# A new order for the 52 tiles of the first input projection

## The chip, the cores and the metric

The kernel runs on one core of a Trainium2 chip. The metric is the device time of one execution in microseconds (us). The engines are named as in the profile: PE is the matrix engine (PEld its weight loads), DVE, ACT and POOL are the vector, scalar and general engines, SP issues the DMAs.

## What is computed

One inference step of a decoder trunk of two layers, for 512 prompt tokens and 8 x 4 sample tokens (544 columns in all), model width 2048. The first layer, in which the change lies:

```
h = x @ w_in
h_sh, gate_a, q_b, k_b, v_b, gate_b, q_m, gate_m = _split(
    h, (A_SHIFT_W, A_WIDTH, B_WIDTH, B_WIDTH, B_WIDTH, B_OUT, M_WIDTH, M_WIDTH))
y_a, s_new = rwkv7_mix(h_sh + (prev - h_sh) * mu, s0, ...)
y_b = combine_by_denominator(outs, lses)      # dilated window attention, 3 groups x 4 heads
y_m = memory_attention(q_m, mkv)              # 4 heads, 256 memory tokens
u = concat([y_a * silu(gate_a), y_b * silu(gate_b), y_m * silu(gate_m)])
x = layer_norm(ALPHA * x + u @ w_out, ln_g, ln_b)
```

The recurrence of rwkv7_mix (12 heads x 64) runs in pairs of heads, so there are six pairs. The second layer (retention and the same memory attention) has a projection, heads and an output projection of its own.

## The kernel before

**Tiles.** Every projection is cut into tiles of 128 output rows. A tile of the first input projection multiplies 16 blocks of weights with the 544 columns in two halves of 272; each product is made of three matmuls (high x high, high x low, low x high), so a tile is 2 x 16 x 3 = 96 matmuls into the PSUM tile m. The stages follow each other on PE: 8 memory tiles, the tile h18 and then the 52 tiles of `ORDER0` (L2212), 32 half tiles of the first output projection (16 blocks of columns for the first half, then 16 for the second; 36 matmuls each), 8 memory tiles, 56 tiles of the second input projection, 32 half tiles of the second output projection.

**Kinds of tiles.** A letter of `ORDER0` takes the next tile of its kind; I number them as they come: r0 to r17 (a pair of heads needs r3p, r3p+1, r3p+2 for p = 0 to 5), q0 to q3 (queries of the memory attention), m0 to m3 (its gates), b0 to b17 (dilated attention: for the first two heads of each group queries b0 to b2, keys b3 to b5, values b6 to b8; for the others b9 to b11, b12 to b14, b15 to b17), a0 to a5 (gates of the six pairs), c0 and c1 (gates of the dilated attention).

**Side jobs.** What a finished tile makes possible is spawned as a job (a generator), with a rank; between main matmuls the program's author-time planner (`pump`, L327) emits instructions of the job of the lowest rank, of equal ranks the one spawned first, that it takes to be ready. The jobs of a pair are `rwkv_pre` (L856, rank 1, spawned by r3p+2), `rwkv_solve` (L1029, rank 0; a forward substitution of 62 short instructions on DVE), `rwkv_chain` (L1113, rank 0; 8 steps, each PE, ACT, PE, ACT, PE, DVE in turn), `rwkv_sample` with `rwkv_norm` (L1180, L1239, rank 3). `b_prompt` for the first two heads (rank 3, after b8) and the others (rank 0, after b17) is the prompt's dilated attention, `b_keys` (rank 3, after b11) and `b_values` (rank 3, after b17) are the sample's. `mem_prompt` and `mem_sample` (rank 4) follow the q tiles. `gate_mul` (rank 4) multiplies a gate with its finished head.

**Pages.** All of this shares 41 pages of on-chip memory (`npages`, L2233), each 128 x 576. A job that opens an account (`open`) waits until so many pages are free beside what others have reserved: `rwkv_pre` 13, given back as a reservation after the fourth step of `rwkv_chain` (`em.close`, L1172; `rwkv_sample` is spawned there, and its first act is the load of rwkv_s), `mem_sample` 10, `b_prompt` 8, `b_keys` 7, `b_values` 9. A finished r tile takes two pages and keeps one (`hsh_done`, L801), a b tile one until its attention is through, a gate one until it is multiplied (`gate_done`, L1280; of a and c gates the page stays as the operand of the output projection; m gates go to DRAM and come back, `u0.reload`, spawned at place 49 of the 52). Where a tile's evacuation finds no free page, `page` (L79) calls `drive` (L339): only side jobs are emitted until one is free, and no main matmul stands in PE's queue in the meantime.

**Output projection.** Its operands are taken in the order in which the gates stand in `ORDER0` (`out_order`, L2217); `mov` (L1883) of a block that isn't ready calls `drive` as well.

Of the kernel before, what the change touches and what calls it, by code (L numbers as in the profile page):

```python
# [2208 lines left out]


MEM0 = (0, 1, 2, 3, 4, 5, 6, 7)
ORDER0 = 'rrqrbbqrqqrrrrrmbrmbbbrbrmbrbmarrbabrarraabbbbbbbcca'  # L2212
ORDER1 = '0000000011111111222222223333333344444444qqqq55555555mmmm'
SPILL1 = (0, 1, 2, 3, 4, 5, 6, 7, 8, 9)

# [1 line left out]
def out_order():  # L2217

    ks0, ks = [], {'a': list(range(6)), 'c': [6, 7], 'm': list(range(8, 12))}
    for ch in ORDER0:  # L2220
        if ch in ks:
            ks0.append(ks[ch].pop(0))
    ks1, left = [], {c: ORDER1.count(c) for c in ORDER1}
    for ch in ORDER1:
        left[ch] -= 1
        if ch == 'm':
            ks1.append(15 - left[ch])
        elif ch != 'q' and left[ch] < 2:
            ks1.append(2 * int(ch) + 1 - left[ch])
    return ks0, ks1  # L2230


def body(nc, tc, A, npages=41, stop=None):  # L2233
    from contextlib import ExitStack
    with ExitStack() as es:
# [92 lines left out]
        ks0, ks1 = out_order()  # L2328
        for ch in ORDER0:
            order.append(kinds[ch].pop(0))  # L2330
# [258 lines left out]
```

## Time and profile before

| | us |
|---|---|
| median of 3 runs | 2276.11 (2273.98 to 2277.71) |
| profiled execution | 2275.39 |
| its span, first to last instruction | 2273.5 |
| PE busy | 2164.6 (95%) |
| DVE busy | 1295.1 (57%) |
| ACT busy | 986.5 (43%) |
| POOL busy | 295.2 (13%) |
| granted clock, mean | 0.981 |

The 40 slices of the page are 56.8 us each. The places where a tile begins were counted off in the trace: 96 matmuls into m to a tile (36 to a half tile of the first output projection). A stretch's row of busy times also counts the matmuls that overlap its edges.

### The profile page before, as it was taken

How to read it: one execution, taken by the hardware profiler on the slowest of the kernel's cores; microseconds unless marked ns; L12 is line 12 of the kernel's file. 1: busy time of each engine (PE TensorE's matmuls, PEld its weight loads, DVE VectorE, ACT ScalarE, POOL GpSimd, SP SyncE). 2: the span in 40 equal slices, each digit the busy share in tenths (PEclk: the TensorE clock that was granted, in tenths of full speed). 3: DMA queues.
4: the chain of work that ended last, by engine and by line, in shares of the span. 5: the costliest groups of instructions: out<-in, count | busy, mean ns of one | idle time of the engine just before them, and what ended most of it. 6: DMA issues, size and time to landing. Idle time of an engine off the chain costs nothing. (4 is left out here: it accounts for less than half of the span.)

```text
span 2273.5 us, 46101 instructions
## 1 busy us (share of the span) xinstructions
PE 2164.6 (95%) x18537; PEld 2082.0 (92%) x18537; DVE 1295.1 (57%) x2718; ACT 986.5 (43%) x2310; POOL 295.2 (13%) x445
## 2 busy tenths in 40 slices
PE   8999999879998999989989999999999999999996
PEld 8999898868888988879989999999999999999995
DVE  6367468636856766357796344444444433437686
ACT  6344453346454444444657232323233242235464
POOL 0000000000000000005482000000000000003574
PEclk9999999979999999989999999999999999999998
DMA  9322633312323325557568243434343425345662
GB/s 336 98 73 79 205 97 91 105 34 82 112 75 93 91 83 164 171 188 241 166 198 279 92 135 103 135 103 135 102 136 97 142 76 204 120 167 189 208 212 98
DMA packets 149716, 313.46 MB, mean 138 GB/s; under 512 B 39377, under 2 KB 48537, under 8 KB 149501
## 3 DMA queue, kind: packets, MB, share of 16 engines
q1 hardware_dynamic: 149500, 310.51, 42.0%
q8 instruction: 146, 2.39, 0.4%
q14 instruction: 70, 0.57, 0.1%
HBM read 271.38 MB, written 39.07 MB: 137 GB/s over the span
## 5 line engine op out<-in xcount | busy, mean ns | idle before, releaser
L194 PE MATMUL m<-xh,wh 128*128 128x272 f32 (+1 forms) x4448 | 1320.3, 297 | 8.0 <-ACT wh L227 3.2
L194 PE MATMUL m<-xh,wl 128*128 128x272 f32 (+1 forms) x4448 | 1288.2, 290 | 9.3 <-DVE wl L235 9.1
L194 PE MATMUL m<-xl,wh 128*128 128x272 f32 (+1 forms) x4448 | 1284.9, 289 | 3.4 <-DVE xl L235 3.4
L194 PEld LDWEIGHTS m<-xh,wh 128*128 128x128 f32 x4448 | 843.3, 190 | 21.1 <-issue 9.0
L194 PEld LDWEIGHTS m<-xh,wl 128*128 128x128 f32 x4448 | 841.4, 189 | 12.2 <-DVE wl L235 12.0
L194 PEld LDWEIGHTS m<-xl,wh 128*128 128x128 f32 x4448 | 843.6, 190 | 6.5 <-DVE xl L235 3.7
L235 DVE TENSOR_TENSOR wl<-wr,wh 128x512 fp32r<-128x512 f32 (+1 forms) x752 | 547.3, 759 | 441.1 <-ACT wh L227 434.9
L227 ACT ACTIVATE wh<-wr 128x512 fp32r<-128x512 f32 (+1 forms) x752 | 419.3, 605 | 248.6 <-PE m L194 237.5
L235 POOL TENSOR_TENSOR P<-P,P 128x272 f32<-128x272 f32 (+1 forms) x242 | 243.5, 1028 | 897.6 <-ACT P L227 735.4
L194 PE MATMUL s<-P,P 128*128 128x128 f32 (+12 forms) x3712 | 318.7, 285 | 39.5 <-ACT P L227 23.8
L194 PEld LDWEIGHTS s<-P,P 128*32 128x32 f32 (+6 forms) x3712 | 243.1, 146 | 86.3 <-ACT P L227 32.1
L227 ACT ACTIVATE P<-m 128x272 f32<-128x272 f32 (+3 forms) x265 | 99.7, 393 | 504.9 <-PE m L194 501.1
L235 DVE TENSOR_TENSOR P<-P,P 128x544 f32<-128x544 f32 (+24 forms) x576 | 280.0, 497 | 54.8 <-ACT P L227 40.3
L227 ACT ACTIVATE P<-s 64x64 f32<-64x64 f32 (+9 forms) x581 | 159.6, 291 | 306.5 <-PE s L194 121.1
L227 ACT ACTIVATE P<-P 64x64 f32<-64x64 f32 (+5 forms) x284 | 124.4, 451 | 125.0 <-POOL P L235 71.5
L240 DVE SCALAR_TENSOR_TENSOR P<-P,m 128x272 f32<-128x272 f32 x116 | 50.3, 434 | 127.4 <-ACT P L227 92.5
L284 POOL MEMSET P<- 128x576 f32 (+6 forms) x104 | 28.9, 293 | 480.4 <-PE s L194 280.9
L194 PE MATMUL m<-P,wh 128*128 128x256 f32 x352 | 67.6, 293 | 7.6 <-ACT wh L227 7.0
L209 PE MATMUL s<-cst,P 128*128 128x128 f32 (+2 forms) x409 | 62.2, 275 | 3.2 <-DVE P L235 2.2
L194 PEld LDWEIGHTS m<-P,wh 128*128 128x128 f32 x352 | 56.9, 198 | 8.5 <-ACT wh L227 7.2
L267 DVE TENSOR_REDUCE P<-P 102x1 f32<-102x2 f32 (+16 forms) x193 | 60.9, 315 | 6.7
L240 DVE SCALAR_TENSOR_TENSOR P<-P,s 128x512 f32<-128x512 f32 x66 | 44.0, 684 | 33.0 <-PE s L194 33.0
(69 smaller groups left out, 890.6 us busy)
## 6 DMA issues: line engine op xcount, KB each, us to landing
wr<-w_in SPq DMA_DIRECT2D x218, 512.0 KB
wr<-w_out SPq DMA_DIRECT2D x64, 512.0 KB
wr<-w_out SPq DMA_DIRECT2D x64, 384.0 KB
wr<-w_mem SPq DMA_DIRECT2D x26, 512.0 KB
P<-ret_s SPq DMA_DIRECT2D x48, 256.0 KB
o_ret_s<-P SPq DMA_DIRECT2D x48, 256.0 KB
P<-dk SPq DMA_DIRECT2D x36, 256.0 KB
P<-dv SPq DMA_DIRECT2D x36, 256.0 KB
```

The lines of the kernel that those rows point to most:

```text
L194: self.nc.tensor.matmul(out, lhsT, rhs, start=start, stop=stop, skip_group_check=True)
L209: self.nc.tensor.transpose(out, in_, ident)
L227: self.nc.scalar.activation(out, in_, func, **kw)
L235: e.tensor_tensor(out, a, b, op=op)
L240: self.nc.vector.scalar_tensor_tensor(out, a, s, b, op0=op0, op1=op1)
L267: self.nc.vector.tensor_reduce(out, a, axis=AX.X, op=op)
L284: e.memset(out, v)
```

## The change

One constant, the order of the tiles:

```
-ORDER0 = 'rrqrbbqrqqrrrrrmbrmbbbrbrmbrbmarrbabrarraabbbbbbbcca'
+ORDER0 = 'rrrbqrqbrqqrrrrbmbrbbbmbmrbrrrmrarabbcrracbbbababbba'
```

The counts of the letters are the same, so the same 52 tiles are computed. The places of the tiles of which the prediction speaks:

| tile | place before | place after |
|---|---|---|
| r2, r5, r8 (last of pairs 0, 1, 2) | 4, 12, 15 | 3, 12, 15 |
| r11, r14, r17 (last of pairs 3, 4, 5) | 25, 33, 40 | 28, 32, 40 |
| q0, q1, q2, q3 | 3, 7, 9, 10 | 5, 7, 10, 11 |
| m0, m1, m2, m3 | 16, 19, 26, 30 | 17, 23, 25, 31 |
| r9, r10 | 18, 23 | 19, 26 |
| b6, b7, b8 | 24, 27, 29 | 22, 24, 27 |
| b11, b17 | 43, 49 | 43, 51 |
| c0, c1 | 50, 51 | 38, 42 |
| a3, a4, a5 | 41, 42, 52 | 46, 48, 52 |

The order of the operands in the first output projection follows: before m0 to m3, a0 to a4, c0, c1, a5; after m0 to m3, a0, a1, c0, a2, c1, a3, a4, a5. The rows of w_out are laid out to match, in loads of the same number and size.

## Rows read from the trace of the kernel before

**Rows 1.** The profile page: the span of the profiled execution.

```profile
span 2273.5 us, 46101 instructions
```

**Rows 2.** Busy times by stretch (the stretch in us, its length, then busy us and instructions of PE, PEld, DVE, ACT and POOL, granted clock, DMA share, GB/s): the 53 tiles of the first projection with the first half tile behind them, and the second input projection.

```profile
56.60:1022.70 966.10, 899.99 (x8269) 846.22 (x8268) 594.43 (x1519) 440.91 (x1171) 42.64 (x176) 0.97 0.34 108
...
1237.10:2051.40 814.30, 814.30 (x6611) 794.23 (x6610) 332.40 (x643) 258.42 (x566) 14.16 (x17) 1.00 0.38 127
```

**Rows 3.** The same view for shorter stretches, in this order: r0; r7; r10 and b6; r11; m2; m3; r14; the nine tiles a3 to b17; c0 and c1; the first half tile of the output projection.

```profile
68.87:80.90 12.03, 12.03 (x98) 12.03 (x97) 3.50 (x6) 4.46 (x10) 0.53 (x4) 1.00 0.25 87
267.40:288.80 21.40, 21.16 (x232) 19.27 (x231) 11.45 (x33) 9.34 (x33) 0.58 (x4) 1.00 0.67 237
...
413.30:440.80 27.50, 27.42 (x271) 26.81 (x270) 13.94 (x52) 12.14 (x38) 1.54 (x10) 1.00 0.44 128
440.80:485.60 44.80, 31.17 (x232) 28.08 (x232) 23.97 (x60) 16.30 (x56) 2.29 (x7) 0.70 0.17 42
485.60:512.40 26.80, 22.23 (x159) 20.79 (x158) 11.34 (x28) 13.68 (x53) 0.88 (x3) 0.94 0.19 62
...
564.90:591.00 26.10, 21.67 (x198) 19.29 (x197) 21.81 (x52) 11.37 (x23) 0.94 (x3) 0.93 0.41 127
615.60:632.70 17.10, 17.10 (x171) 16.36 (x170) 15.03 (x30) 8.17 (x20) 2.25 (x4) 1.00 0.24 68
...
756.70:919.20 162.50, 152.91 (x1472) 143.69 (x1471) 100.38 (x258) 76.77 (x213) 6.36 (x27) 0.99 0.42 129
919.20:972.50 53.30, 52.15 (x707) 45.43 (x707) 24.05 (x60) 20.32 (x67) 2.75 (x5) 1.00 0.38 129
...
993.60:1022.70 29.10, 19.22 (x430) 15.88 (x429) 13.11 (x45) 11.27 (x22) 1.17 (x4) 0.71 0.90 317
```

**Rows 4.** Timeline of PE inside r11 (start us, us, engine, line, operation, count; in brackets the idle time before it and what ended it): the last main matmul of its first half, and the next work after it.

```profile
446.66 0.29 PE L194 MATMUL m<-xh,wl 128*128 128x272 f32 x1
...
458.16 0.80 PE L194 MATMUL s<-P,P 128*128 128x128 f32 x2 [8.80 <-ACT P L227]
```

**Rows 5.** Timeline of DVE (same columns): the first and the last instruction of a forward substitution, and what stood behind it; then of ACT, the wait that this ended.

```profile
431.50 0.15 DVE L235 TENSOR_TENSOR P<-P,P 102x2 f32<-102x2 f32 x1
...
456.44 0.52 DVE L267 TENSOR_REDUCE P<-P 102x11 f32<-102x352 f32 x1
456.99 0.58 DVE L240 SCALAR_TENSOR_TENSOR P<-s,P,P 64x64 f32<-64x64 f32 x2
...
457.66 0.45 ACT L227 ACTIVATE P<-s 64x64 f32<-64x64 f32 x2 [9.60 <-DVE P L240]
```

**Rows 6.** Timeline of SP's DMA issues: P<-lora, the first load of a pair after its 13 pages are granted (pairs 0, 1, 3, 4, 5); P<-rwkv_s, the first act after the reservation is given back (pairs 0, 1, 3, 4, 5); o_rwkv_p, the end of the chain (pairs 0, 4, 5); yad<-P, the end of the pair (pairs 0, 3, 4, 5).

```profile
119.06 0.43 SPq L288 DMA_DIRECT2D P<-lora  x1
289.21 0.38 SPq L288 DMA_DIRECT2D P<-lora  x1
...
515.51 0.39 SPq L288 DMA_DIRECT2D P<-lora  x1
646.70 0.38 SPq L288 DMA_DIRECT2D P<-lora  x1
774.23 0.93 SPq L288 DMA_DIRECT2D P<-lora  x1
...
253.45 0.38 SPq L288 DMA_DIRECT2D P<-rwkv_s  x1
467.46 0.42 SPq L288 DMA_DIRECT2D P<-rwkv_s  x1
668.30 0.38 SPq L288 DMA_DIRECT2D P<-rwkv_s  x1
819.81 0.38 SPq L288 DMA_DIRECT2D P<-rwkv_s  x1
960.27 0.38 SPq L288 DMA_DIRECT2D P<-rwkv_s  x1
...
283.84 0.55 SPq L288 DMA_DIRECT2D o_rwkv_p<-P  x1
851.02 1.68 SPq L288 DMA_DIRECT2D o_rwkv_p<-P  x2
948.51 0.48 SPq L288 DMA_DIRECT2D o_rwkv_p<-P  x1
...
311.40 0.33 SPq L288 DMA_DIRECT2D yad<-P  x1
773.24 0.42 SPq L288 DMA_DIRECT2D yad<-P  x1
900.00 0.33 SPq L288 DMA_DIRECT2D yad<-P  x1
1012.30 0.33 SPq L288 DMA_DIRECT2D yad<-P  x1
```

**Rows 7.** Timelines at the end of the stage: PE's first scores of the second b_prompt; ACT's last evacuation of it; PE's last block of the first half tile, which is a5; and from the groups by line, b_values' matmuls inside that half tile (busy us, mean ns, idle before them).

```profile
945.96 0.69 PE L194 MATMUL d<-P,P 64*32 64x256 f32 x16
...
988.62 0.59 ACT L227 ACTIVATE P<-s 128x512 f32<-128x512 f32 x1
...
1021.41 0.59 PE L194 MATMUL m<-xl,wh 128*128 128x272 f32 x1 [3.40 <-DVE xl L235]
...
L194 PE MATMUL s<-P,P 128*32 128x64 f32 x384 | 11.8, 275 | 6.5 <-DVE P L259 3.5 <-DMA P<-dv 2.8
```

## Prediction

> **What bounds the kernel now.** I read the span first (2273.5 us [rows 1]), then the busy times by stretch, then the same view tile by tile, and where a tile was too long, the timeline of the engine that waited and of the one it waited for. The time is PE's: outside the first projection it hardly waits (the second projection, 814.3 us long, has PE busy for all of it at full clock), so a new order of the first projection's tiles can only win or lose inside the 966.1 us of that stage, where PE is busy for 900.0 at a mean clock of 0.97 [rows 2]. A tile without side work lasts 12.03 us [rows 3], and 53 of them are 638 us; the rest is side work, which the change leaves as it is, and waiting, 66.1 us by the idle time in this row [rows 2]. Two places stand out. r11 lasts 44.8 us at a clock of 0.70 with as many matmuls as r7, which lasts 21.4 [rows 3]: 23.4 us too long. And the first half tile of the output projection lasts 29.1 us at 0.71 [rows 3] and ends in a wait for a5 [rows 7].
>
> **Why r11 waits.** By the code all 41 pages are then taken or reserved. Before r11: pairs 1 and 2 hold 14 each (13 and a value page), h18 one, the sample queries one, q2 and q3 two, b0 to b6 seven, r9 and r10 two: 41. r11's first half ends at 446.95 [rows 4] and needs two more, so main matmuls stop until pair 1 gives back its reservation at 467.46 [rows 6]: 20.5 us. It takes so long because the chain of pair 1 stands on DVE behind pair 2's forward substitution (431.50 to 456.96), and ACT waits 9.60 us for it [rows 5].
>
> **Why the stage ends late.** At r17 the same count gives: h18 one, sample queries one, first dilated head pair one, three a gates, b9 and b10 two, r15 to r17 three, pair 4 14: 25, and four for pair 3, which is in its norm. Twelve are free, pair 5 needs 13. So its first load is issued at 774.23, just behind pair 3's last store at 773.24 [rows 6], and the stage ends a pair's life later: pair 5's last store is issued at 1012.30 (238.1 us), a5 reaches PE at 1021.41 [rows 6, 7].
>
> **The change, part by part.** No instruction is added or removed. Where the planner now puts each side instruction the trace of before can't show; the bounds below stand for that. Each moved tile takes its 96 matmuls, its weight loads, evacuations, POOL copies and stores along. POOL is busy for 42.64 of 966.1 us [rows 2] and an issue on SP takes 0.3 to 0.9 us [rows 6]; I put the moved issues at nothing, under SP's idle time, and at most a few of them, some 2 us, if they meet a weight load. The new layout of w_out costs nothing: same loads. c0 and c1 now come 12 and 9 places earlier and hold two pages to the end; no engine instruction waits on them, but the count at the end is two higher.
>
> *The page wall moves from r11 to m1.* After b6, now at place 22, the count is: pairs 28, h18 and sample queries two, q1 to q3 three, b0 to b6 seven, r9 one: 41 again. m1's first half needs one more. That is two places before the old wall, so r10's and b6's 27.5 us earlier [rows 3]: at about 419.4. What decides is when pair 1 gives way. It opens when pair 0's chain ends (289.21 behind 283.84 [rows 6]), and r2 now comes one place earlier, 12.0 us by a bare tile: 277.2. From opening to giving way pair 0 took 134.4, pair 1 178.3 and pair 3 152.8 [rows 6]. Pair 2 can't open earlier (the memory samples follow q3, one place later, and hold 10 pages), so the two pairs stand further apart and pair 1 should meet less of pair 2's forward substitution; I take pair 3's 152.8: 430. The wait is 10.6 us instead of 20.5, a gain of 10 (bounds: none left, 20.5 gained; with 178.3 it lasts until 455.5, 36 us, 15.6 lost). Of the tiles behind, m2 (26.8 us, fewer matmuls than r7) and m3 (26.1) are 5.4 and 4.7 too long [rows 3], while three pairs share DVE and ACT; I take half of these 10, 5 us (bounds 0 and 10). Together 15 us by r14.
>
> The Trainium skill (TensorE: Matmul & The Clock Gate, Terms) puts the penalty of a lowered clock at the time under it times half. Of r11's 44.8 us 60% were at the lower level by the mean of 0.70 [rows 3], which by that rule is 13.4 us lost; what the rows leave for the clock is less, 23.4 less 13.6 of idle time, 9.8, since much of the low stretch is idle anyway. By the page the shorter wait would give 2 us more.
>
> *Pair 5 opens at another signal.* r14 comes at place 32 instead of 33. With the same tiles done by then as before by 615.6 [rows 3], it ends at 600; pair 4 opens 14.0 us later as before (646.70 behind 632.7 [rows 3, 6]): 614. Pair 3 comes three places later and is no longer through at r17; instead pair 4 gives back its reservation, 152.8 later, at 767 (bounds by 134.4 and 178.3: 749 and 793). Pair 5 then opens at 767 instead of 774: 7 earlier (25 earlier to 19 later).
>
> *Pair 5's life.* From the chain's end to the last store pair 0 took 27.6, pair 4 49.0, pair 5 63.8 us, and pair 5's sample began 11.8 after its chain's end, where pair 4's began 31.2 before it [rows 6]: b_keys, spawned earlier at the same rank, and the second b_prompt stood ahead of it. b_keys keeps place 43, but the pages it waits for come free with pair 4, earlier; I take pair 4's 49.0, 15 less (bounds 0 and 36). a5 then reaches PE at 1021.4 less 7 less 15: 999.
>
> *The second b_prompt comes two tiles later.* b17 moves from place 49 to 51. Before, place 51 ended at 972.5 [rows 3]; less 15 and less some 10 us of b_prompt's own matmuls that lay ahead of it, b17 now ends at 947 (bounds 928: the old 919.2 and two bare tiles, less 15; and 957). b_prompt ended at 989.2, 70.0 after b17 and 43.3 after its first scores [rows 3, 7]; the 27 us between were partly a wait for pages that pair 5 should have given back by now. I take 54: 1001 (bounds 971 and 1027). Its gate c1 is the ninth of the twelve operands, so the output projection waits for it about as long as for a5. The later of the two is 1001, 20 us before 1021.4.
>
> *What was hidden comes out.* b_values' 384 matmuls lay in that old wait, 11.8 us [rows 7]. They need b_prompt's pages, so most of them now come behind it, between main matmuls: 10 us back (bounds 0 and 11.8).
>
> **Sum.** 2275.4 (profiled execution: the span and 1.9 us around it; 0.7 under the median) less 20 plus 10: 2265.
>
> **Rivals.** *The wall is worse at m1* (ends slower). If pair 1 still needs 178.3 us, main matmuls stop at 419 until 455.5 with two tiles fewer done: 15.6 us lost there, nothing won at m2 and m3, all later openings shifted by it. 2275.4 plus 15.6 is 2291. It decides as soon as giving way takes more than 163 us from opening (419.4 plus 20.5 less 277.2). For it: pairs 1 and 4 took 178.3 and 173.1 [rows 6], DVE serves pair 2 in its order [rows 5]; against it: the larger distance of the pairs. The Trainium skill (TensorE: Matmul & The Clock Gate, Architectural detail, its lines on queue depths) calls DVE a strict first-in, first-out queue, and the 9.60 us in [rows 5] agree; by that rule any overlap of a chain with a forward substitution costs the same again, wherever the order puts it.
>
> *The tail eats it* (no change). The wall is won, but b17's late place is not made up: 70 us after 957 is 1027, a5's gain is wasted, and b_values' covered part gives back what the middle won. For it: two tiles fewer behind b17, two pages more held. 2276.
>
> *Both waits go* (more gain). Pair 1 gives way before m1 needs it, by 412 with pair 0's 134.4, and pair 5's sample begins on time: b_prompt's lower bound and a5's then meet near 985, 36 us gained, 4 of b_values back: 2243.
>
> **How the numbers follow.** Forecast 2265 with 0.50 (its own range 2250 to 2274), worse wall 0.24, no change 0.16, both waits gone 0.10. About 0.2%, 4.6 us, is what a measurement of this kernel can tell from no change. Of the forecast nine tenths, and the large gain, are faster: 0.56; the no-change case and some of the forecast's edge: 0.18; the worse wall and the tail's bad edge: 0.26. The range takes in the large gain and the worse wall: 2243 to 2291.
>
> **What would show it.** Tile m1 should have the longest idle time of the middle of the stage, and less than r11's 13.6; pair 1's load of rwkv_s near 430; pair 5's first load before 774; b_prompt's last evacuation and a5's first matmul close to each other near 1000; b_values' matmuls among the output projection's half tiles. I am wrong if r11 still holds the longest wait, if pair 5 opens after 790, or if the gain lies outside this stage.

## The result, and the profile after

| | us |
|---|---|
| median of 4 runs | 2244.22 (2243.55 to 2246.62) |
| before, beside it | 2276.08 (2273.98 to 2277.71) |
| ratio | 0.9862 [0.9845, 0.988] |
| span of the profiled execution | 2242.9 (before 2273.5 [rows 1]) |

32 us were gained where 11 were forecast. Busy times by stretch of the changed kernel (columns as in [rows 2, 3]): the first projection with the first half tile behind it; the second projection; m1; m2; r11; the first half tile of the output projection.

```profile
56.60:991.60 935.00, 887.15 (x8141) 838.54 (x8140) 591.88 (x1507) 441.39 (x1168) 42.91 (x176) 0.98 0.35 110
1205.90:2020.10 814.20, 814.20 (x6612) 794.02 (x6611) 331.35 (x640) 257.70 (x565) 14.19 (x17) 1.00 0.38 127
418.70:431.90 13.20, 13.20 (x109) 13.20 (x108) 10.25 (x41) 4.69 (x14) 0.40 (x3) 1.00 0.31 101
445.80:470.70 24.90, 20.82 (x178) 19.10 (x176) 10.76 (x27) 12.39 (x39) 1.86 (x3) 0.93 0.39 108
504.40:530.30 25.90, 23.96 (x233) 21.33 (x231) 14.98 (x32) 12.54 (x40) 2.25 (x9) 0.93 0.22 72
968.50:991.60 23.10, 19.72 (x407) 16.73 (x406) 13.28 (x45) 10.29 (x25) 1.18 (x4) 0.85 0.90 317
```

The stage lasts 935.0 us instead of 966.1 [rows 2], and what lies behind it 0.5 longer, so the gain of 30.6 in the span is all in this stage. PE's idle time there fell from 66.1 to 47.8. r11 lasts 25.9 instead of 44.8 [rows 3] at a clock of 0.93 instead of 0.70, and **m1, where the wall was forecast, doesn't wait at all**.

*What the gain is made of.* At the end of the ninth half tile both kernels have done the same side work (3344 side matmuls counted off since the program's beginning), and the changed one is 30.4 ahead (1034.6 against 1065.0). PE's idle time in the stage by then is 47.8 instead of 66.1, 18.3 less, and the time at the lower clock level (1.2 GHz), counted off in the trace, 44.4 instead of 68.3, 23.9 less. The Trainium skill (TensorE: Matmul & The Clock Gate, Terms) prices a halved clock at half the time under it; by that, 18.3 and half of 23.9 are 30.3. The agreement is no proof, since part of the time at the lower level is idle time and so counted twice: PE is busy for only 38.7 of the 44.4 us, and for 53.0 of the 68.3. Half of this difference is 7.2, and with the idle time it makes 25.4; the other 5 us are shorter busy time that the trace doesn't put down to the clock. Of the 30.4, 22.6 are there by place 26 (both with 919 side matmuls).

*Why m1 runs through.* Timeline of PE in the changed kernel, the last matmul of m1's first half, and of ACT around m1:

```profile
425.51 0.29 PE L194 MATMUL m<-xh,wl 128*128 128x272 f32 x1
...
427.66 0.45 ACT L227 ACTIVATE P<-s 64x64 f32<-64x64 f32 x2 [6.34 <-DVE P L240]
428.13 0.40 ACT L227 ACTIVATE P<-m 128x272 f32<-128x272 f32 x1
...
432.07 0.40 ACT L227 ACTIVATE P<-m 128x272 f32<-128x272 f32 x1 [1.79 <-PE m L194]
```

m1's first half is done on PE at 425.8. The first row of ACT ends the fourth step of pair 1's chain at 428.1 (by the count of the chain's instructions), which is when the pair gives way. The next row evacuates m1's first half into the page it needed. The second half keeps PE busy meanwhile, until 431.9, so the 2.3 us left of the wait are hidden.

*Why pair 1 gives way so early.* Timeline of DVE, the steps of pair 1's chain and the first instruction of pair 2's forward substitution (102 rows): in the kernel before, where the substitution is the one of [rows 5], the first step; in the changed kernel the first three steps, the substitution's beginning and the fourth step.

```profile
424.33 0.60 DVE L246 TENSOR_SCALAR P<-s,P 64x64 f32<-64x64 f32 x2 [5.34 <-PE s L194]
...
403.94 0.60 DVE L246 TENSOR_SCALAR P<-s,P 64x64 f32<-64x64 f32 x2
...
410.02 0.58 DVE L240 SCALAR_TENSOR_TENSOR P<-s,P,P 64x64 f32<-64x64 f32 x2 [2.31 <-PE s L194]
...
416.24 0.58 DVE L240 SCALAR_TENSOR_TENSOR P<-s,P,P 64x64 f32<-64x64 f32 x2
...
420.95 0.15 DVE L235 TENSOR_TENSOR P<-P,P 102x2 f32<-102x2 f32 x1
...
426.98 0.58 DVE L240 SCALAR_TENSOR_TENSOR P<-s,P,P 64x64 f32<-64x64 f32 x2
```

Before, the chain's first step stands 7.2 us ahead of the substitution, and the second comes only behind it, at 456.99 [rows 5]. In the changed kernel the first step stands 17.0 us ahead, three steps are through when the substitution begins, and the fourth runs within it. The give-way at 470.6 before is 428.1 now.

Timeline of SP in the changed kernel, the issues that answer to [rows 6]: first loads of pairs 1 to 5, chain ends (pairs 0, 2, 3), pair 1's load of rwkv_s, last stores of pairs 3 and 5.

```profile
278.48 1.18 SPq L288 DMA_DIRECT2D o_rwkv_p<-P  x2
279.76 0.54 SPq L288 DMA_DIRECT2D P<-lora  x1
...
321.98 0.38 SPq L288 DMA_DIRECT2D P<-lora  x1
...
462.53 0.42 SPq L288 DMA_DIRECT2D P<-rwkv_s  x1
...
549.75 1.11 SPq L288 DMA_DIRECT2D o_rwkv_p<-P  x2
552.65 0.38 SPq L288 DMA_DIRECT2D P<-lora  x1
...
597.54 0.33 SPq L288 DMA_DIRECT2D P<-lora  x1
...
744.46 1.12 SPq L288 DMA_DIRECT2D o_rwkv_p<-P  x2
745.68 0.52 SPq L288 DMA_DIRECT2D P<-lora  x1
...
816.40 0.34 SPq L288 DMA_DIRECT2D yad<-P  x1
...
941.92 0.32 SPq L288 DMA_DIRECT2D yad<-P  x1
```

By these loads pairs 1 and 2 now begin 42.2 us apart instead of 22.6 (in the kernel before 289.21 [rows 6] and 311.82), and pair 5 is through at 941.9, 70 earlier. The end of the stage, timelines of PE (first scores of the second b_prompt), ACT (its last evacuation), DVE (its gate, c1) and PE (the output projection's wait):

```profile
943.51 1.34 PE L194 MATMUL d<-P,P 64*32 64x256 f32 x24
...
986.00 0.60 ACT L227 ACTIVATE P<-s 128x512 f32<-128x512 f32 x1 [2.44 <-PE s L194]
...
987.43 0.43 DVE L240 SCALAR_TENSOR_TENSOR P<-P,P 128x272 f32<-128x272 f32 x1
...
988.28 0.39 PE L194 MATMUL m<-xl,wh 128*128 128x272 f32 x1 [1.00 <-DVE xl L235]
```

Before, the last wait was for a5, pair 5's gate, and ended at 1021.41 [rows 7]; now it is for c1 and ends at 988.28. The second b_prompt itself ends only 2.6 earlier (986.6 against 989.2): before, it wasn't the later of the two. From its first scores it takes 43.1 us, as before (43.3 [rows 7]); what is gone is the wait between b17 and these scores, 1.7 us instead of 26.8.

### The profile page after: what moved, and what is told of

Same layout as the page of the kernel before. It is cut to its first block, busy times and chain, and to the rows that moved or that the text cites. A ratio compares the mean times of both kernels' runs of the same rounds, so it can differ in the third digit from the quotient of the medians.

```text
span 2242.9 us, 46091 instructions
## 1 busy us (share of the span) xinstructions
PE 2156.3 (96%) x18537; PEld 2078.8 (93%) x18537; DVE 1292.6 (58%) x2718; ACT 987.2 (44%) x2310; POOL 295.0 (13%) x445
## 5 line engine op out<-in xcount | busy, mean ns | idle before, releaser
L194 PEld LDWEIGHTS m<-xh,wh 128*128 128x128 f32 x4448 | 843.9, 190 | 17.0 <-issue 10.7
L194 PE MATMUL s<-P,P 128*128 128x128 f32 (+11 forms) x3712 | 313.6, 281 | 31.3 <-ACT P L227 18.1
L194 PEld LDWEIGHTS s<-P,P 128*32 128x32 f32 (+5 forms) x3712 | 240.0, 143 | 72.8 <-ACT P L227 23.6
L235 DVE TENSOR_TENSOR P<-P,P 128x544 f32<-128x544 f32 (+20 forms) x576 | 279.8, 497 | 43.3 <-ACT P L227 34.6
L227 ACT ACTIVATE P<-s 64x64 f32<-64x64 f32 (+10 forms) x581 | 160.0, 292 | 292.9 <-PE s L194 129.8
```

What stands on the lines that cost most here:

```text
L194: self.nc.tensor.matmul(out, lhsT, rhs, start=start, stop=stop, skip_group_check=True)
L227: self.nc.scalar.activation(out, in_, func, **kw)
L235: e.tensor_tensor(out, a, b, op=op)
```

## The experiments

All times are against the kernel before, run beside them (medians 2276.9 to 2278.0). A result gives the median in us, its ratio to before and, in brackets, the 95% interval of the ratio. "Lead" is the time by which a kernel is ahead of before in its trace when both have finished the same number of places; where their side work differs it is said. In the changed kernel the lead is 44.0 at r17 (with 48 side matmuls fewer) and 31.1 at the stage's end.

**Halves of the order.** New places 1 to 40 with a tail near the old one; and the old 40 with the new tail.

```
+ORDER0 = 'rrrbqrqbrqqrrrrbmbrbbbmbmrbrrrmrarabbcrraaabbbbbbbca'   # e1
+ORDER0 = 'rrqrbbqrqqrrrrrmbrmbbbrbrmbrbmarrbabrarrccbbbababbba'   # e2
```

> The first 40 places in the new order (to r17), the last 12 in the old manner (a2, a3, a4, b11 to b17, c1, a5). Theory M, that the gain comes from the middle (the page wait at r11 is gone, and with it idle time and low clock): 2236 to 2250, about the changed kernel's time, and at r17's end some 44 us ahead of the kernel before. Rival T, that the later places make it (gates put between the last b tiles, c0 and c1 early): 2262 to 2276.

> The first 40 places in the old order, the last 12 in the new manner (c0, c1, b11 to b13, a3, b14, a4, b15 to b17, a5). Theory M: 2270 to 2282, no gain, the wait at r11 as before (20 us). Rival T: 2246 to 2260.

e1: 2250.6 us, 0.9886 [0.987, 0.9903]. e2: 2282.21, 1.0024 [1.0014, 1.0033]; r11 there still takes 44.2 us. The gain is made in the first 40 places: e1's trace, of a run of 2244.85, is 30.0 ahead at the end of the ninth half tile, where the changed kernel's is 30.4. The new tail by itself costs 0.2%.

**One suspected cause each.** r2 one place earlier and nothing else; and the chain's rank raised above the forward substitution's, in the old order.

```
+ORDER0 = 'rrrqbbqrqqrrrrrmbrmbbbrbrmbrbmarrbabrarraabbbbbbbcca'   # e3
-    em.spawn(rwkv_chain(g, p), 0)                                 # e4
+    em.spawn(rwkv_chain(g, p), -1)
```

> The order before with one exchange: r2 at place 3, q0 at place 4. Theory S, that pair 1's earlier start decides (it gives its pages back before pair 2's forward substitution occupies DVE): the wait at r11 falls from 20 us to under 8, time 2255 to 2264. Rival D, that the request for pages decides (r10 and r11 come later, m1 and m2 free pages before them): the wait stays, 2271 to 2280.

> The order before; the chain of a pair gets rank -1 instead of 0, so its instructions are emitted ahead of another pair's forward substitution. Theory F, that pair 1's chain stands on DVE behind pair 2's substitution: pair 1's load of rwkv_s moves from 467 to under 448, r11 lasts under 30 us, time 2252 to 2264. Rival L, that the pair simply needs its life whatever the queue: the load stays within 460 to 470 and the time within 2270 to 2280.

e3: 2275.5, 0.9997 [0.9988, 1.0007]; pair 1's first load is issued at 290.5, pair 2's at 306.3, and r11 takes 43.7 us. e4: 2275.99, 0.9997 [0.9987, 1.0006]; r11 takes 34.3 and the lead at place 26 is 11.5 us, but at r17 the kernel is 6.5 behind (with 80 side matmuls more done) and its time is that of before. Serving the chain first is worth 10 us at the wall, and nothing at the end.

**Places 1 to 17 against the rest.** The first 17 places hold the same tiles in both orders, so they can be crossed.

```
+ORDER0 = 'rrrbqrqbrqqrrrrbmrmbbbrbrmbrbmarrbabrarraabbbbbbbcca'   # e5
+ORDER0 = 'rrqrbbqrqqrrrrrmbbrbbbmbmrbrrrmrarabbcrracbbbababbba'   # e6
```

> Places 1 to 17 as in the new order, places 18 to 52 as before (r10, r11, m2 and the whole tail keep their old places). Theory U (supply): the wall at r11 goes because pair 1 opens some 25 us earlier, ahead of the ten pages of the memory samples, so the first 17 places alone lift it: pair 1's first load near 280 instead of 289, r11 under 30 us, at place 26 some 15 to 22 us ahead of before, and a total of 2250 to 2262. Theory D (demand): the wall goes because r10 and r11 ask for their pages later; these stand where they stood, so r11 still takes over 40 us and the total is 2270 to 2278.

> Places 1 to 17 as before (the same 17 tiles in the old order), places 18 to 52 as in the new order. Theory U (supply): pair 1 opens late, so the wall comes back, now at m1, the tile that asks for the 42nd page: m1 takes 25 to 45 us instead of 13.2, at place 26 at most 8 us ahead of before, total 2262 to 2278. Theory D (demand): r10 and r11 ask later, so no tile of places 18 to 28 waits over 5 us and the total is within 6 us of the changed kernel's 2244.

e5: 2272.09, 0.9979 [0.9968, 0.9991]. Busy times by stretch of e5: r11, then b9.

```profile
447.40:464.10 16.70, 16.65 (x138) 16.38 (x136) 9.39 (x21) 10.95 (x35) 0.90 (x3) 1.00 0.27 62
607.80:647.50 39.70, 30.25 (x317) 27.17 (x315) 19.93 (x44) 18.55 (x55) 2.07 (x6) 0.79 0.21 56
```

e6: 2297.3, 1.0096 [1.0078, 1.0114]. Busy times of m1 in e6:

```profile
414.30:474.40 60.10, 32.87 (x303) 28.85 (x302) 32.76 (x99) 19.08 (x69) 1.82 (x10) 0.72 0.19 52
```

In e5 r11 doesn't wait though it stands where it stood, so theory D (demand) falls; in e6 m1 takes 60.1 us with 27 idle, the wall at the tile forecast for it. But both missed their expected totals. e6 came 19 above the upper end, with a wait longer than expected. e5 loses what it won: its lead of 30 at place 28 (22 side matmuls fewer) is 13 at r17 and none at the stage's end, in a trace that is of a run of 2279.1 and has 4 us of that behind the stage. Alone the first part gives 5 us and the rest costs 20; together they give 32.

**Pages.** The changed order with 40 pages.

```
-def body(nc, tc, A, npages=41, stop=None):
+def body(nc, tc, A, npages=40, stop=None):
```

> The changed kernel's order with 40 pages instead of 41 (one operand less; nothing else of the kernel is changed). By the count of pages the new order just fits: 41 of 41 are taken or reserved after b6. Theory P (pages make the wall): with 40 a tile near b6, m1 or b7 waits 8 to 25 us for pair 1 and the clock falls there; through place 26 the kernel is 8 to 20 us behind the changed one, total 2250 to 2266. Rival E (engines): the wait at r11 was that of busy DVE and ACT and the pages only went with it; then one page less moves no more than 3 us and no tile of places 20 to 26 waits over 5 us.

e7: 2284.33, 1.0041 [1.0025, 1.0057]. Busy times of e7: b6, m1, b15.

```profile
404.10:440.80 36.70, 18.35 (x140) 16.94 (x139) 24.37 (x74) 9.11 (x34) 0.47 (x3) 0.85 0.16 50
440.80:463.00 22.20, 21.99 (x200) 20.56 (x201) 7.56 (x19) 11.91 (x41) 1.28 (x5) 0.87 0.38 107
872.90:943.20 70.30, 54.68 (x823) 43.88 (x821) 21.40 (x67) 19.26 (x72) 1.74 (x7) 0.85 0.55 174
```

One page less brings the wall back, at b6 (36.7 us instead of 14.8, 18 of them idle): the kernel is 28.6 behind the changed one at place 26 (with 70 side matmuls more done), and 40 at the end, with b15 at 70.3 us instead of 31.9. The wait is one for pages, and the new order fits 41 with nothing to spare. The size was missed: 8 to 20 expected.

**The first 17 places without the move of r2.** As e5, with r2 at place 4 as before and b0 at 3.

```
+ORDER0 = 'rrbrqrqbrqqrrrrbmrmbbbrbrmbrbmarrbabrarraabbbbbbbcca'   # e8
```

> As the run with places 1 to 17 new, but r2 keeps place 4 (b0 goes to 3): the memory queries come later, pair 0 doesn't come earlier. Theory U2 (both are needed: pair 0 must give way before the memory samples open): pair 1's first load after 290, a wait of over 10 us between places 18 and 26, total 2268 to 2282. Rival Q (the late queries alone, since r2 alone was shown to do nothing): pair 1's first load before 283, no such wait, total as with places 1 to 17 new, within 4 us.

e8: 2269.59, 0.9963 [0.995, 0.9975]. Busy times of e8: r11, then b17.

```profile
439.30:452.30 13.00, 13.00 (x107) 13.00 (x106) 12.35 (x28) 3.09 (x9) 0.38 (x3) 1.00 0.33 102
863.30:936.00 72.70, 55.47 (x818) 44.73 (x816) 18.68 (x58) 24.99 (x78) 1.58 (x7) 0.86 0.56 181
```

Both theories had it wrong in part. Pair 1's first load is as late as before (289.45), and yet there is no wall: r11 takes 13.0. So an early first load of pair 1 isn't what is needed. What the runs without a wall share is the distance of pairs 1 and 2 where they meet, on DVE: their forward substitutions begin 71 to 74 us apart in e8, e5 and the changed kernel, and 56 to 57 apart in the four runs with a wall. So the first step of pair 1's chain stands 17 to 18 us ahead of pair 2's substitution, and not 4 to 9. By the code pair 2 is later because the memory samples, which hold ten pages, come later; no run moves them alone. e8's lead is 35 at r17 (equal side work); most of it goes in b17, a tile of 72.7 us of which 17.2 are idle.

| run | pair 1, pair 2 first load | apart | chain's first step ahead of pair 2's substitution | pair 1's fourth step ends | longest tile, places 18 to 28 |
|---|---|---|---|---|---|
| before | 289.2, 311.8 | 22.6 | 7.2 | 470.6 | r11 44.8 |
| e3 | 290.5, 306.3 | 15.8 | 4.1 | 470.8 | r11 43.7 |
| e4 | 291.6, 314.2 | 22.6 | 7.2 | 462.1 | r11 34.3 |
| e6 | 292.6, 315.2 | 22.6 | 8.5 | 462.8 | m1 60.1 |
| e8 | 289.5, 331.5 | 42.0 | 17.8 | 437.1 | b7 22.3 |
| e5 | 280.5, 322.7 | 42.2 | 17.5 | 430.3 | m2 23.0 |
| changed | 279.8, 322.0 | 42.2 | 17.0 | 428.1 | r11 25.9 |

The first loads can come later than their pairs open (e12 and e13 below), so the column on DVE is the safer one.

**Two neighbours.** The changed order with b8 and r11 exchanged.

```
-ORDER0 = 'rrrbqrqbrqqrrrrbmbrbbbmbmrbrrrmrarabbcrracbbbababbba'
+ORDER0 = 'rrrbqrqbrqqrrrrbmbrbbbmbmrrbrrmrarabbcrracbbbababbba'   # e9
```

> The changed kernel with two neighbours exchanged: r11 at place 27, b8 at place 28 (the new order has b8 before r11, the old one r11 four places before b8). Theory Q (who opens first): with b8 first, the first b_prompt gets its 8 pages before pair 3 takes 13, is through by 557 and gives back 17; with r11 first, pair 3 opens first and b_prompt waits for its pages. Then pair 3's first load comes before 535 instead of 552.65, b_prompt's first instruction after 570 instead of 511, r11's own surroundings are no slower (place 28 within 5 us), a tile between places 32 and 37 waits for pages over 8 us, and the total is 2255 to 2280. Rival N (neighbours don't matter, since both are finished by place 28 and the same jobs follow): total within 4 us of 2244.

e9: 2282.29, 1.0017 [1.0005, 1.003]: **one exchange of neighbours takes back the whole gain.** Pair 3's first load comes at 505.62 instead of 552.65 (its first fill on POOL at 507.97 instead of 528.52), the first b_prompt runs from 560 to 640 instead of 511 to 557 (from its first work on DVE), and pair 2's last store waits until 636.93 instead of 573.02. At place 28 e9 is 3.4 ahead of the changed kernel (with 90 side matmuls fewer done), then tiles wait; busy times of e9 for b10 and a2 (13.4 and 20.6 us in the changed kernel):

```profile
671.50:700.30 28.80, 22.29 (x145) 21.11 (x143) 19.47 (x55) 8.72 (x26) 0.49 (x3) 0.82 0.20 65
741.90:778.90 37.00, 23.25 (x206) 21.28 (x206) 18.89 (x41) 18.94 (x45) 1.42 (x6) 0.72 0.22 61
```

Theory Q held in its mechanism: who opens first decides. Its sizes were missed: b_prompt began 10 us earlier than expected, no tile of places 32 to 37 was idle for 8 us (b10, the longest, for 6.5), and the total lies 2 above the range. A b_prompt that goes ahead is through in 46 us and gives back 16 pages (seven of its 8, and the nine b tiles); a pair that goes ahead holds 13 for 150 or more, and b_prompt then lasts 80. The old order had r11 before b8 too, and e5 kept that.

**How far the new order must reach, and the end.** Places 1 to 31 new and then the old rest; and the changed order with a4 and a5 behind all b tiles.

```
+ORDER0 = 'rrrbqrqbrqqrrrrbmbrbbbmbmrbrrrmarbabrarraabbbbbbbcca'   # e10
+ORDER0 = 'rrrbqrqbrqqrrrrbmbrbbbmbmrbrrrmrarabbcrracbbbabbbbaa'   # e11
```

> Places 1 to 31 as in the new order, then the old order for what is left (a0, then a r and b tiles, a's, the b tiles in one row, c0, c1, a5). Theory Q: the wall at r11 is gone and b_prompt is through before r14 asks, so, other than with 17 new places, nothing waits up to place 36 and the lead over before at place 40 is 25 to 45 us instead of 13; the old tail costs some of it: total 2248 to 2264. Rival (places 32 to 52 must be new too: the lead is lost at a page wait in the tail as with 17 places): total 2266 to 2278.

> The changed kernel with a3 at place 46 as it is, but a4 and a5 at the end and the b tiles in front of them (b17 at place 50 instead of 51). Theory L: in the changed kernel the second b_prompt, which can only start after b17, is what the output projection waits for last; one place earlier it ends some 10 us earlier, and the total is 2236 to 2243. Rival K: what lies behind b17 is work that must be done in any case (b_prompt, b_values, their matmuls), so an earlier b17 only moves it from the output projection into a4 and a5, total 2243 to 2250; and if the tail's tiles now ask for pages before pair 5 gives way, more than 2250.

e10: 2269.81, 0.9959 [0.9944, 0.9974]: the lead at r17 is 34.9 (with 38 side matmuls fewer), as theory Q says, and 6.4 at the stage's end, as its rival says. Pair 5 ends at 1006.5 there. e1, which differs from e10 in places 32 to 40 and in little behind them, keeps 18 us more. e11: 2251.07, 0.9878 [0.9863, 0.9892], slower than the changed kernel: the second b_prompt ends at 970, but pair 5 at 993.1, and the stage at 1000.4 instead of 991.6. Theory L falls: with b17 earlier, pair 5 is the later of the two.

**Two readings of the forecast.** The loads of P<-lora on POOL's queue, in the kernel before and in the changed one (order on PE, DVE and ACT as it was):

```
-    em.dma(lw, g.A['lora'][:, 128 * p:128 * p + 128])
+    em.dma(lw, g.A['lora'][:, 128 * p:128 * p + 128], 'gpsimd')
```

> The kernel before, with the six loads of a pair's first operand (P<-lora) issued from POOL's queue instead of SP's; the order of work on PE, DVE and ACT is unchanged. Theory V (SP's order): the pairs were open earlier, and the load stood behind a store of an older pair that waited for its data; then pair 5's load is issued near 758 instead of 774 (pair 3's near 487 instead of 515.5), and pair 5's PE work after it can't start much earlier than its place in PE's order: total 2268 to 2276. Rival W (pages, the forecast's reading): the load still comes at 772 or later, total within 2 us of before.

> The changed kernel with the same loads on POOL's queue. Theory V: the loads of pairs 1, 3 and 5 come at 263, 528 and 728 instead of 279.8, 552.7 and 745.7; since the order on PE is fixed and it has little idle time there, the total falls by 0 to 6 us (2238 to 2244). If SP's wait for older stores held up the pairs, and through them the stage's end, more: 2225 to 2238.

Just before this load a pair fills one of its pages on POOL. Timeline of POOL in the kernel before, the fills of pairs 3 and 5, and in the changed kernel that of pair 5; of SP in the kernel before, ahead of the load at 774.23 [rows 6]; of POOL in e12, and of SP there:

```profile
486.50 0.59 POOL L284 MEMSET P<- 128x576 f32 x1
...
757.92 0.83 POOL L284 MEMSET P<- 128x576 f32 x2
...
728.06 0.87 POOL L284 MEMSET P<- 128x576 f32 x2 [3.68 <-DVE P L235]
...
762.79 3.72 SPq L288 DMA_DIRECT2D td<-P  x3
...
770.45 2.74 SPq L288 DMA_DIRECT2D P<-td  x6
...
758.25 0.57 POOL L284 MEMSET P<- 128x576 f32 x1
758.77 0.54 POOL L288 DMA_DIRECT2D P<-lora  x1
...
773.51 0.42 SPq L288 DMA_DIRECT2D yad<-P  x1
```

e12: 2278.08, 1.0003 [0.9994, 1.0013]. Theory V holds for the load, rival W for the total. Pair 5 has its pages at 758, right behind r17's end at 757.0, and so it has in the kernel before (fill at 757.92, r17's end at 756.7). There its load only stood in SP's queue, behind pair 4's stores and loads of td: the stores waited until 762.78 for pair 4's forward substitution, and the loads until 770.38 for the stores to land. Pair 3's last store stood in the same row and wasn't what waited; DVE had finished its data at 765.4. And the 15 us are worth nothing: PE's order is the same in both, and in the kernel before PE waits only 1.1 us for this load. Pair 3's load is held on SP too, from 486.80 (e12) to 515.51 [rows 6]. e13: 2251.09, 0.9885 [0.987, 0.99], loads at 263.4, 526.8 and 726.4, the stage's end at 991.8 as in the changed kernel (991.6). Its total is above the range of theory V, by 6.6 us in the traces, all behind the stage: 4.9 of them lie at the beginning of the second output projection, where e5 and e7, with the loads on SP, lose 4 us too, so the queue isn't their cause; what is stays open.

Pair 5's sample with the first rank, in the kernel before and in e10:

```
-                em.spawn(rwkv_sample(g, p), 3)
+                em.spawn(rwkv_sample(g, p), 3 if p < 5 else -1)
```

> The kernel before, with the sample of pair 5 given the first rank instead of rank 3 (the other pairs as they are). Theory L (the later of pair 5's last store and the second b_prompt's end sets the stage's end; before it is pair 5, 1012 against 989): pair 5's last store comes before 985, b_prompt becomes the later, at 990 to 1005, and the total falls by 5 to 18 us: 2258 to 2271. Rival Z (what stands behind is PE work to be done in any case): pair 5 earlier, total 2272 to 2277.

> Places 1 to 31 new and the old rest, as in the run of 2269.8, with the sample of pair 5 given the first rank. There pair 5 was last (1006 against b_prompt's 983). Theory L: pair 5's last store before 975, the later of the two near 985 to 990, total 2250 to 2262. Rival Z: 2266 to 2271.

e14: 2269.94, 0.9975 [0.9963, 0.9987]. Timeline of SP in e14: the sample's first load, and pair 5's last store.

```profile
921.22 1.42 SPq L288 DMA_DIRECT2D P<-rwkv_s  x1
...
1004.89 0.33 SPq L288 DMA_DIRECT2D yad<-P  x1
```

The sample begins 39 us earlier than in [rows 6] and the pair ends 7 earlier, not 27. e15: 2264.35, 0.9939 [0.9922, 0.9955], pair 5's last store at 1002.9 instead of 1006.5. The rank accounts for 5 to 7 us of what an old tail loses (28.7 in e10, from r17 to the ninth half tile); the totals fell nearly where Theory L put them, the pair's end did not, so it explains only that part.

No run beats the changed kernel.

## Why the prediction was wrong

The direction and the stage were right; two terms of the sum were mis-sized and two signals were misread. **The steps that failed are the 20 us by which the stage was to end earlier, which measured 31.1, and the 10 us that b_values was to cost, which measured 0.5.** The time of the third rival, 2243, is what came, but not by its reason: pair 1 gave way at 428.1, not by 412.

- *The second b_prompt*, the later end, by which the 20 was taken, ended at 986.6, not 1001. b17 ended at 941.8 instead of 947 (5.2 of the 14.4), and from there it took 44.8 instead of 54 (9.2). Its work was sized rightly, 43 us from the first scores; the wait before them, of which I left half, was gone. By then pair 5 had given everything back (last store 941.92). That the later of b_prompt and a5 sets the end held.
- *b_values* was to cost 10 us, with most of its matmuls behind the wait. 256 of its matmuls still lie in the first half tile, inside the wait for c1 now, where 384 lay before; the other 128 come out behind it, and the eight half tiles that follow take 43.0 us instead of 42.2.
- *The wall.* The count of 41 of 41 after b6 was right (e7). What failed is the time at which it is met. I put the moment when main matmuls stop at 419.4, by subtracting the two tiles' old durations. But the order before m1 carries more side work (743 side matmuls by the end of b6, 649 at the same place before), so m1's first half ends at 425.8, and the tile's second half, which needs no further page, hides the rest. Wait 0 instead of 10.6. By place 26 the gain was 22.6, where 15 were forecast by r14.
- *Pair 1's give-way*, forecast at 430 and measured at 428.1, came right by luck, since two errors offset each other. The 152.8 of pair 3 was read from a load that SP held; pair 3 had its pages at 486.50 by POOL's fill, so it took 181.8, about as long as pairs 1 and 4. And the opening, put at 277.2, was at 263 by e13's load, 14 earlier. Nor does the load of rwkv_s tell the give-way, as [rows 6] has it: it comes 3.1 before the fourth step's end in the kernel before (467.46, 470.6), and at 462.53, 34 behind it, in the changed one, so the sign "near 430" failed. The reason for the early give-way was in the text, the larger distance of pairs 1 and 2; the traces show that distance on DVE in every run without the wall.
- *The worse wall at m1* is real: e6 has it, at m1, with 60 us and 2297.3 against the rival's 2291. There the chain's first step is 8.5 us ahead of pair 2's substitution. But an overlap doesn't cost the same wherever it lies, as the rival had it: before, the second step came 32.7 us behind the first; in the changed kernel the fourth, which overlaps the substitution too, comes 10.7 behind the third.
- *Pair 5's signal.* Neither pair 3's end nor pair 4's give-way opens pair 5. In the kernel before it opens as soon as r17 is done, and the load I read it by was held by SP's order. In the changed kernel r17 ends 44.0 earlier, at 712.7, but POOL's fill for pair 5 stands 15.4 behind that, behind a wait for DVE, so pair 5 begins 29.9 earlier; what holds it there I didn't follow. The step named the wrong cause, and by it forecast 7 us earlier for a load that came 28.5 earlier.
- *Pair 5's life* was 196 us from load to last store instead of 223, so a5's path was through long before 999.

So the stage's end moved by 31.1 instead of 20, and 0.5 came back instead of 10: 2275.4 less 31.1 plus 0.5 is 2244.8. The step that was not in the text at all is the swap of b8 and r11: it lets the first b_prompt open before pair 3, and without it (e9) all the rest is worth nothing.

What stays open: why exactly the old places 32 to 52 give back most of a lead of 30 to 35 us (at place 28 in e5, at r17 in e8 and e10). The runs show where (long tiles b9 and b17 in e5, b17 in e8, b11 to b13, b17 and c0 in e10, each of 22 to 73 us, and pair 5 ending at 997.6 to 1009.3 in all three), not one cause that could be changed alone.

## What to carry to other kernels

Where jobs share a pool that just fits, the order of asking is the schedule: let the short job that gives back much go ahead of the long one that holds much, and keep two long ones far enough apart that the first gives way before the pool is asked again. Forecast both ends of such a wait, not only the one that was visible, and count what the waiting tile can still do in the meantime. Parts of an order don't add: here minus 5 and plus 20 made minus 32 together.

## What the runs showed of the hardware

A load queued on SP behind stores that still wait for their data, and behind loads that wait for these stores to land, is held with them: 774.23 [rows 6] against 758.77 from POOL's queue (e12). So the issue of a first load doesn't tell when its job was ready; and the earlier load moved nothing (1.0003), since PE had waited only 1.1 us for the late one.
